# Reordering the paged decode of a hybrid decoder step, with operands of VectorE moved to PSUM

## The chip, the core and the metric

The kernel runs on one core of a Trainium2 chip. The metric is the device time of one execution in microseconds (us). TensorE (PE in the profile, PEld for its weight loads), VectorE (DVE), ScalarE (ACT), GpSimd (POOL) and the DMA queues of SyncE (SP) and ScalarE work side by side and meet at semaphores.

## The reference

One inference step of a two-layer decoder, all in float32, for a prompt of 16 + 512 tokens and 8 decode rows of one token each.

- Layer 0: a Mamba-2 mixer (`mamba2_mixer`), `post_norm`, a SwiGLU FFN (1024 to 2816 to 1024), `post_norm`. From its output come one set of keys and values for layer 1.
- Layer 1: differential attention over them (8 heads, two softmax maps each), `post_norm`, a second SwiGLU FFN, `post_norm`.
- The decode rows attend over paged past keys and values: per row 16 pages of 128 tokens, each page 128 x 1024 floats (512 KB) of keys and as much of values, so 128 pages of each, 134 MB in all.

```python
def post_norm(x, sub, w, b): return layer_norm(DEEPNORM_ALPHA * x + sub, w, b)
def swiglu(x, wg, wu, wd):   return (silu(x @ wg) * (x @ wu)) @ wd
def diff_attn_sample(h, k_past, v_past, k_new, v_new, ...):
    s = concat([einsum('bqhcd,bkhcd->bhcqk', q, k_past) * scale, s_new])
    w = softmax(s)[:, :, 0] - lam * softmax(s)[:, :, 1]
    o = w[..., :P] @ v_past + w[..., P:] @ v_new
```

## The kernel before

All 536 tokens (528 of the prompt, 8 decode rows) stand as columns; 1024 features are 8 tiles of 128 partitions. A float32 product is made of three matmuls on rounded halves: each operand is split into a high part (a ScalarE copy into the reduced type) and a low part (operand minus high part), and `unit` issues high-high, high-low and low-high (line 121). `wensure` (180) loads a weight chunk on ScalarE's DMA queue, makes its high part on ScalarE (200) and its low part (202) on the engine that `lo_engine` names: VectorE, and in the phase "attn" GpSimd. Four split chunks are kept.

The stages in order are the mixer, its output product, FFN 0 (`ffn`, 932; two parts of 11 gate/up pairs and 8 down products, at most 512 columns a matmul), the attention (`attention`, 1246; per head three products of keys, values and queries, then a generator `head`), the output product (`out_norm`, 1334), FFN 1 and the last norm. Each FFN's silu output is multiplied by the up product into SBUF (964) and then split there (`split`, 240).

`ln` (271) is a layer norm on column halves: sums over partitions by matmuls with ones, mean copied to SBUF (280), root by Ln and Exp (315); per pair of tiles a subtraction of the mean (288) and a product with the root (290), then per tile the high part on ScalarE (294), the value with weight and bias (303) and the low part (305). Norm 1 (`tight`) has lines 288 to 305 on VectorE and ScalarE; norms 0, 2 and 3 put some of 288, 303 and 305 on GpSimd.

A planner in the program sets the order. `Sched.t` adds a nominal time for each matmul that is emitted; generators (norms, heads, the decode) yield delays and are stepped when that clock passes them. A clock value is a place in the program's order, not a time on the chip. `finish(gen)` runs all that is due until a generator is done. SP's queue runs in the order of emission.

The decode first runs the whole layer 0 for the decode rows by itself (`early`, 1038), beside FFN 0, to get their queries; then `decode` (1154) is stepped every 3.2 of the planner's clock. Step n does key page n: a load into one of three slots (1151), the product with the query row on GpSimd (1191, in place, 128 x 1024), the sum over 64 features on VectorE (1192). It also does value page n - 24: a load into one of three other slots and four matmuls of 32 weight columns (the weights `w` of the row's softmax) into four quarters of the bank `ps_e` (1199; eight instructions in the trace). After 16 key pages a row's softmax is spawned (`dec_softmax`, 1208, four matmul and VectorE steps with yields of 0.6, 0.8 and 2.0); after 16 value pages `dec_out` (1232). The slots lie in the regions R5 and dA, which `out_norm` needs for the split attention output: it calls `S.finish(self.dec_gen)` at its start (1340).

Of the kernel before, what the change touches and what calls it, by code (L numbers as in the profile page):

```python
# [10 lines left out]
F32 = mybir.dt.float32  # L11
# [3 lines left out]
AF = mybir.ActivationFunctionType  # L15
# [21 lines left out]

ES0 = 24

KACT = (6, 7)  # L40
# [70 lines left out]
class Kernel:  # L111
# [68 lines left out]
    def wensure(self, load, split):  # L180
# [14 lines left out]
        while self.wsplit < min(split, len(self.wq)):  # L195
# [5 lines left out]
            eng = self.lo_engine()  # L201
            eng.tensor_tensor(out=lo[:, :n, :mw], in0=r, in1=hi[:, :n, :mw].bitcast(F32), op=ALU.subtract)  # L202
# [68 lines left out]
    def ln(self, t3, s2, q2, li, n, hilo=None, xf_out=None, after=None):  # L271
# [3 lines left out]
        pm, pv = (self.ps("c"), self.ps("d")) if n == NE else (self.ps(self.lnps[0]), self.ps(self.lnps[1]))  # L275
        self.mmf(pm[:, :n], self.ones, s2)
        self.mmf(pv[:, :n], self.ones, q2)
        md = self.sp.tile([P, 260], F32, tag="ln_md", name="ln_md")[:, :n]
        rs = self.sp.tile([P, 260], F32, tag="ln_rs", name="ln_rs")[:, :n]
        mdi = A.activation(md, pm[:, :n], AF.Copy, scale=1.0 / 1024)  # L280
        A.activation(rs, pm[:, :n], AF.Square, scale=1.0 / 1024)
        V.scalar_tensor_tensor(out=rs, in0=pv[:, :n], scalar=1.0 / 1024, in1=rs, op0=ALU.mult, op1=ALU.subtract)
        V.tensor_scalar(out=rs, in0=rs, scalar1=0.0, scalar2=None, op0=ALU.max)
        self.rsqrt(rs, rs, 1.0, mdi)
        for k in range(8):
            if k % 2 == 0:
                t2 = t3[:, k:k + 2, :]
                (G if k >= 4 and n > NE and not self.tight(li) else V).tensor_tensor(
                    out=t2, in0=t2, in1=bc(md, 1, 2), op=ALU.subtract)
                V.tensor_tensor(out=t2, in0=t2, in1=bc(rs, 1, 2), op=ALU.mult)  # L290
            w, b = self.lnw[:, li, k:k + 1], self.lnb[:, li, k:k + 1]
            if hilo is not None:
                hi, lo = hilo(k)
                A.activation(hi, t3[:, k, :], AF.Identity, bias=b, scale=w)
            if xf_out is not None:
                xf = xf_out(k)
            else:
                xf = self.sp.tile([P, LNW], F32, tag="lx", name="ln_xf", bufs=2)[:, :n]
            if (hilo is None and k % 2 == 0) or (self.tight(li) and k in KACT):
                A.activation(xf, t3[:, k, :], AF.Identity, bias=b, scale=w)  # L300
            else:
                E1 = V if self.tight(li) else G
                E1.tensor_scalar(out=xf, in0=t3[:, k, :], scalar1=w, scalar2=b, op0=ALU.mult, op1=ALU.add)  # L303
            if hilo is not None:
                (V if k % 2 == 0 or self.tight(li) else G).tensor_tensor(out=lo, in0=xf, in1=hi.bitcast(F32), op=ALU.subtract)  # L305
            if after is not None:
                after(k, xf)
# [4 lines left out]
    def tight(self, li):  # L312
        return li in (1,)

    def rsqrt(self, out, in_, scale, after=None):

        A = self.nc.scalar
        p = out.partition_size()
        l = A.activation(out, in_, AF.Ln, bias=self.eps[:p, :], scale=scale)
        e = A.activation(out, out, AF.Exp, scale=-0.5)  # L320
# [13 lines left out]
    def build(self):  # L334
        nc, tc = self.nc, self.tc
        with ExitStack() as ctx:
# [5 lines left out]
            self.gi, self.gn = 0, 3  # L342
            self.wi = 0
# [569 lines left out]
    def proj(self, groups, xk, halves, evac, lnf, lasth=None):  # L913
# [3 lines left out]
        for gi, grp in enumerate(groups):  # L917
            last = gi == len(groups) - 1
            chs = [self.wget(nc_) for _, nc_ in grp]
# [12 lines left out]
    def ffn(self, xk, halves, mk_t, lnf, gens, after_first=None, lasth=None, regs=("R0", "R1")):  # L932
# [3 lines left out]
        for part in range(2):  # L936
# [6 lines left out]
            while j < 11:  # L943
# [5 lines left out]
                for hf, (c0, n) in enumerate((lasth or halves) if first else halves):  # L949
# [4 lines left out]
                    for jj, (cg, cu) in zip(grp, chs):  # L954
# [83 lines left out]
    def early(self, t):  # L1038
# [106 lines left out]
        yield 3.0  # L1145
        self.dec_gen = S.spawn(self.decode(), 0.0)
# [7 lines left out]
    def decode(self):  # L1154
        nc, S, i, sp = self.nc, self.S, self.i, self.sp
        V, A, G = nc.vector, nc.scalar, nc.gpsimd
        kslot = self.kslot
        vslot = [self.r5[:, 1, :], self.r5[:, 2, :], self.r5[:, 3, :]]
# [4 lines left out]
        kq, vq = {}, {}  # L1163
        N = 128
# [6 lines left out]
        page = self.page  # L1171
        VL = 24
        w = {}
        sc = None
        qload(0)
        for n in range(N + VL + 1):
            if n < N:
                b, p = divmod(n, 16)
                if p == 8 and b < 7:
                    qload(b + 1)  # L1180
                if p == 0:
                    sc = sp.tile([P, 288], F32, tag="sc", name="sc", bufs=3)
                    V.memset(sc[:, 256:], 0.0)
                if n + 2 < N:
                    page("cache_k", n + 2, kslot[(n + 2) % 3])
            v = n - VL
            if 0 <= v + 2 < N:
                page("cache_v", v + 2, vslot[(v + 2) % 3])
            if n < N:
                kt = kslot[n % 3]  # L1190
                G.tensor_tensor(out=kt, in0=kt, in1=qslot[b % 2], op=ALU.mult)  # L1191
                V.reduce_sum(sc[:, 16 * p:16 * p + 16], kt.rearrange("p (c d) -> p c d", d=64), axis=AX)  # L1192
            if v >= 0 and v < N:
# [502 lines left out]
```

## Time and profile before

| | us |
|---|---|
| median of 3 runs (1810.86 to 1817.8) | 1814.14 |
| the profiled execution's own time | 1822.45 |
| its span, first to last instruction | 1820.6 |
| VectorE / ScalarE / GpSimd busy | 1170.4 / 731.7 / 567.0 |
| pages read by the decode | 256 of 512 KB |

The profiled execution is 8.3 us above the median. In the profile's windows FFN 0 with the decode beside it runs from about 605 to 980 us, the first head of the attention from about 1000, the last key/value/query product ends at 1319, the output product and norm 2 run to about 1430, FFN 1 to 1795. A busy share is an average over such stages; which wait ends last is read stage by stage.

### The profile page before, as it was taken

The numbers are of one execution on the slowest core, as the hardware profiler recorded it, in microseconds if no ns is written. First come the engines' busy times: TensorE is split into PE (matmuls) and PEld (weight loads), VectorE is DVE, ScalarE is ACT, GpSimd is POOL, SyncE is SP. The second block draws the span as 40 slices with busy tenths as digits, with TensorE's granted clock in tenths as the row PEclk, the third lists the DMA queues.
The fourth block names the chain that finished last, engine by engine and source line by source line (L and its number), as shares of the span: only waits on it lengthen the run. The fifth ranks groups of instructions, "written<-read, shape, count | busy, mean of one in ns | idle before, by whom it ended". The sixth has DMA issues, their size and how long they took to land.

```text
span 1820.6 us, 32047 instructions
## 1 busy us (share of the span) xinstructions
PE 1671.1 (92%) x12234; PEld 1408.3 (77%) x12234; DVE 1170.4 (64%) x1837; ACT 731.7 (40%) x1521; POOL 567.0 (31%) x402
## 2 busy tenths in 40 slices
PE   7899999979998989999997687999987899999996
PEld 7798888957775766666665464679976899999995
DVE  5498988934452699876678958757678533443334
ACT  6866765442442221222223222455644432223223
POOL 0010011001240586555588485312225400000025
PEclk9999999989999999999998697999998999999998
DMA  5665565596979779989898577761211222332221
GB/s 174 175 226 175 181 216 187 132 258 214 328 253 339 231 243 344 342 318 328 314 321 308 199 285 253 267 210 57 72 45 67 70 93 71 92 116 93 76 81 55
DMA packets 156800, 355.49 MB, mean 195 GB/s; under 512 B 23509, under 2 KB 74118, under 8 KB 156518
## 3 DMA queue, kind: packets, MB, share of 16 engines
q1 hardware_dynamic: 116902, 228.26, 37.6%
q10 hardware_dynamic: 36944, 116.59, 19.0%
q0 software_dynamic: 2800, 8.60, 1.4%
q8 instruction: 96, 1.57, 0.3%
q14 instruction: 58, 0.48, 0.1%
HBM read 337.07 MB, written 16.52 MB: 194 GB/s over the span
## 4 chain that ended last, share of the span: by engine, by line
PE 59%; DVE 17%; DMA 10%; ACT 5%; POOL 4%; issue 4%; SPq 1%; POOLq 0%; ACTq 0%; DVEq 0%
PE ps_g L121 48%; PE ps_e L125 3%; DMA st<-in_state_ssm 3%; DVE sc L1192 2%; PE ps_a L125 2%; DVE wlo L202 2%; PE ps_d L125 2%; DMA out_conv_s<-cv 1%; PE ps_c L125 1%; DMA dd<-in_cache_k 1%; POOL dd L1191 1%; POOL ln_xf L303 1%; ACT acsb L752 1%; DMA r<-in_w_out 1%; DMA r<-in_cache_v 1%
## 5 line engine op out<-in xcount | busy, mean ns | idle before, releaser
L200 ACT CAST whi<-raw 128x1024 fp32r<-128x1024 f32 (+3 forms) x243 | 234.8, 967 | 483.5 <-PE ps_g L121 419.2
L202 DVE TENSOR_TENSOR wlo<-raw,whi 128x1024 fp32r<-128x1024 f32 (+2 forms) x211 | 279.3, 1325 | 188.4 <-ACT whi L200 185.9
L1191 POOL TENSOR_TENSOR dd<-dd 128x1024 f32<-128x1024 f32 x85 | 216.3, 2550 | 97.7 <-DMA dd<-in_cache_k 88.1
L121 PE MATMUL ps_g<-xhi,whi 128*128 128x268 f32 (+1 forms) x656 | 196.8, 300 | 16.5 <-ACT xhi L242 9.2
L121 PE MATMUL ps_g<-x3hi,whi 128*128 128x260 f32 x704 | 200.4, 285 | 3.7 <-ACT sgw L958 3.2
L121 PE MATMUL ps_g<-x3lo,whi 128*128 128x260 f32 x704 | 199.6, 284 | 1.3 <-POOL x3lo L305 1.3
L121 PE MATMUL ps_g<-x3hi,wlo 128*128 128x260 f32 x704 | 199.2, 283 | 0.0
L121 PE MATMUL ps_g<-xhi,wlo 128*128 128x268 f32 (+1 forms) x656 | 194.4, 296 | 0.0
L121 PE MATMUL ps_g<-xlo,whi 128*128 128x268 f32 (+1 forms) x656 | 193.9, 296 | 0.1
L121 PE MATMUL ps_g<-x1hi,whi 128*128 128x512 f32 (+1 forms) x384 | 147.9, 385 | 4.1 <-ACT sgw L958 4.1
L121 PE MATMUL ps_g<-x1lo,whi 128*128 128x512 f32 (+1 forms) x384 | 148.5, 387 | 3.3 <-POOL x1lo L305 3.2
L121 PE MATMUL ps_g<-x1hi,wlo 128*128 128x512 f32 (+1 forms) x384 | 147.2, 383 | 0.0
L121 PEld LDWEIGHTS ps_g<-xhi,whi 128*128 128x128 f32 (+1 forms) x656 | 125.1, 191 | 24.3 <-ACT xhi L242 9.2
L1191 POOL TENSOR_TENSOR r<-r,dd 128x1024 f32<-128x1024 f32 x43 | 107.1, 2490 | 118.0 <-DMA dd<-scr_q 75.5
L121 PEld LDWEIGHTS ps_g<-x3hi,whi 128*128 128x128 f32 x704 | 133.0, 189 | 4.4 <-ACT sgw L958 3.6
L121 PEld LDWEIGHTS ps_g<-x3lo,whi 128*128 128x128 f32 x704 | 133.4, 189 | 1.5 <-POOL x3lo L305 1.5
L121 PEld LDWEIGHTS ps_g<-x3hi,wlo 128*128 128x128 f32 x704 | 133.7, 190 | 0.0
L121 PEld LDWEIGHTS ps_g<-xlo,whi 128*128 128x128 f32 (+1 forms) x656 | 125.3, 191 | 6.2 <-issue 5.1
L121 PEld LDWEIGHTS ps_g<-xhi,wlo 128*128 128x128 f32 (+1 forms) x656 | 125.0, 191 | 5.7 <-issue 5.1
L121 PE MATMUL ps_g<-hlo,whi 128*128 128x260 f32 (+2 forms) x400 | 126.7, 317 | 0.0
L121 PE MATMUL ps_g<-hhi,whi 128*128 128x260 f32 (+2 forms) x400 | 126.2, 316 | 0.0
L121 PE MATMUL ps_g<-hhi,wlo 128*128 128x260 f32 (+2 forms) x400 | 126.2, 316 | 0.0
(523 smaller groups left out, 4148.1 us busy)
## 6 DMA issues: line engine op xcount, KB each, us to landing
r<-in_cache_v SPq DMA_DIRECT2D x128, 512.0 KB, 5.3
dd<-in_cache_k SPq DMA_DIRECT2D x85, 512.0 KB, 4.6
raw<-in_w_gate ACTq DMA_DIRECT2D x44, 512.0 KB, 4.3
raw<-in_w_up ACTq DMA_DIRECT2D x44, 512.0 KB, 6.8
r<-in_cache_k SPq DMA_DIRECT2D x43, 512.0 KB, 6.5
raw<-in_w_in ACTq DMA_DIRECT2D x40, 512.0 KB, 3.6
raw<-in_w_down ACTq DMA_DIRECT2D x32, 384.0 KB, 3.2
raw<-in_w_down ACTq DMA_DIRECT2D x32, 320.0 KB, 4.7
```

Source lines behind the costliest of these rows:

```text
L121: return self.nc.tensor.matmul(out, lhsT=l, rhs=r, start=start, stop=stop)
L125: return self.nc.tensor.matmul(out, lhsT=l, rhs=r, start=start, stop=stop)
L200: nc.scalar.copy(hi[:, :n, :mw], r)
L202: eng.tensor_tensor(out=lo[:, :n, :mw], in0=r, in1=hi[:, :n, :mw].bitcast(F32), op=ALU.subtract)
L303: E1.tensor_scalar(out=xf, in0=t3[:, k, :], scalar1=w, scalar2=b, op0=ALU.mult, op1=ALU.add)
L752: A.activation(x, x, AF.Relu, scale=-1.0, bias=b)
L1191: G.tensor_tensor(out=kt, in0=kt, in1=qslot[b % 2], op=ALU.mult)
L1192: V.reduce_sum(sc[:, 16 * p:16 * p + 16], kt.rearrange("p (c d) -> p c d", d=64), axis=AX)
```

## The change

The decode walks all 128 key pages first, one page every 2.5 of the planner's clock, in five slots (the three of before and two that held values). A row's score tile gets a place of its own for all eight rows. Then come all 128 value pages, two every 4.8, in seven slots (those five and the two of the query rows), the four matmuls of a page with one priority. The softmax yields longer delays.

While `wps` is set (from the decode's start to the last group of FFN 0) the low part of a weight chunk is made in two halves: ScalarE copies a half of the raw chunk to PSUM bank a or b, and VectorE subtracts with that operand. The gate-times-up product is written into the PSUM bank of the up product and split from there, in both FFNs. The norms read mean and root from PSUM and fold weight and bias in another way; only the bias of half the tiles of norm 3 stays on GpSimd. The phase "attn", and with it GpSimd's low parts, begins after head 0's products.

```diff
+KY, VY = 2.5, 4.8
@@ wensure
-            eng = self.lo_engine()
-            eng.tensor_tensor(out=lo[:, :n, :mw], in0=r, in1=hi[:, :n, :mw].bitcast(F32), op=ALU.subtract)
+            if self.wps:
+                for x in range(0, n, 4):
+                    y = min(x + 4, n)
+                    pw = self.ps("ab"[x // 4])[:, :P * (y - x)].rearrange("p (k c) -> p k c", c=P)
+                    nc.scalar.copy(pw, r[:, x:y, :])
+                    nc.vector.tensor_tensor(out=lo[:, x:y, :], in0=pw, in1=hi[:, x:y, :].bitcast(F32), op=ALU.subtract)
+            else:
...
@@ ln
-        mdi = A.activation(md, pm[:, :n], AF.Copy, scale=1.0 / 1024)
...
-        self.rsqrt(rs, rs, 1.0, mdi)
+        self.rsqrt(pv, rs, 1.0, sqi, mid=rs)
+        for k in range(0, 8, 2):
+            t2 = t3[:, k:k + 2, :]
+            V.scalar_tensor_tensor(out=t2, in0=bc(pm, 1, 2), scalar=-1.0 / 1024, in1=t2, op0=ALU.mult, op1=ALU.add)
         for k in range(8):
-            if k % 2 == 0:
-                t2 = t3[:, k:k + 2, :]
-                (G if k >= 4 and n > NE and not self.tight(li) else V).tensor_tensor(
-                    out=t2, in0=t2, in1=bc(md, 1, 2), op=ALU.subtract)
-                V.tensor_tensor(out=t2, in0=t2, in1=bc(rs, 1, 2), op=ALU.mult)
             w, b = self.lnw[:, li, k:k + 1], self.lnb[:, li, k:k + 1]
+            t = t3[:, k, :]
+            V.scalar_tensor_tensor(out=t, in0=t, scalar=w, in1=pv, op0=ALU.mult, op1=ALU.mult)
             if hilo is not None:
                 hi, lo = hilo(k)
-                A.activation(hi, t3[:, k, :], AF.Identity, bias=b, scale=w)
...
+                A.activation(hi, t, AF.Identity, bias=b)
+                V.scalar_tensor_tensor(out=lo, in0=t, scalar=b, in1=hi.bitcast(F32), op0=ALU.add, op1=ALU.subtract)
+            else:
                 xf = xf_out(k)
...
+                if small or k % 2 == 0:
+                    A.activation(xf, t, AF.Identity, bias=b)
+                else:
+                    G.tensor_scalar(out=xf, in0=t, scalar1=b, scalar2=None, op0=ALU.add)
@@ ffn
-                        V.tensor_tensor(out=sg, in0=sg, in1=pu[:, :n], op=ALU.mult)
+                        V.tensor_tensor(out=pu[:, :n], in0=sg, in1=pu[:, :n], op=ALU.mult)
                         hh, hl = hk(jj)
-                        self.split(hh[:, c0:c0 + n], hl[:, c0:c0 + n], sg)
+                        self.split(hh[:, c0:c0 + n], hl[:, c0:c0 + n], pu[:, :n])
@@ decode (rewritten)
+        kslot = self.kslot + [self.r5[:, 1, :], self.r5[:, 2, :]]
+        N, R = 128, 5
...
+        for n in range(N):
+            b, p = divmod(n, 16)
...
+            if n + R - 1 < N:
+                self.page("cache_k", n + R - 1, kslot[(n + R - 1) % R])
+            kt = kslot[n % R]
+            G.tensor_tensor(out=kt, in0=kt, in1=qslot[b % 2], op=ALU.mult)
+            V.reduce_sum(w[b][:, 16 * p:16 * p + 16], kt.rearrange("p (c d) -> p c d", d=64), axis=AX)
+            yield KY
...
+        vslot = [kslot[n % R] for n in range(N - R, N)] + qslot
+        R = 7
+        for n in range(R - 2):
+            self.page("cache_v", n, vslot[n])
+        yield 6.0
+        for n in range(N):
...
+            if n + R - 2 < N:
+                self.page("cache_v", n + R - 2, vslot[(n + R - 2) % R])
...
+            pr = self.tc.cur_priority
+            for j in range(4):
+                self.tc.cur_priority = pr
+                self.mmf(pe[32 * j:32 * j + 32, :256], w[bv][:, 16 * pv:16 * pv + 32],
+                         vt[:, 256 * j:256 * j + 256], start=pv == 0, stop=pv == 15, share=4)
...
+            if n % 2 == 1:
+                yield VY
@@ dec_softmax, dec_out: yields 0.6, 0.8, 2.0 become 2.5, 2.5, 4.0; 1.0 becomes 2.0
@@ attention
-        self.phase = "attn"
...
                     for wi in range(3):
                         kvq(h, wi, chs[wi], hf)
+                self.phase = "attn"
```

## Rows read from the trace of the kernel before

**Rows 1.** The page, part 1: busy us, share of the span, instructions.
```profile
PE 1671.1 (92%) x12234; PEld 1408.3 (77%) x12234; DVE 1170.4 (64%) x1837; ACT 731.7 (40%) x1521; POOL 567.0 (31%) x402
```

**Rows 2.** Windows by stage: us, busy us and (instructions) per engine; clock, DMA share, GB/s.
```profile
605.00:755.00 150.00, 139.76 (x674) 102.30 (x673) 136.40 (x116) 35.57 (x46) 109.44 (x43) 0.99 0.84 294
755.00:955.00 200.00, 200.00 (x1085) 136.53 (x1084) 138.75 (x131) 55.40 (x70) 126.47 (x54) 1.00 0.90 320
980.00:1055.00 75.00, 49.52 (x320) 36.26 (x320) 67.93 (x83) 27.02 (x49) 42.18 (x19) 0.70 0.64 222
1055.00:1130.00 75.00, 54.61 (x420) 39.96 (x419) 61.67 (x103) 17.52 (x46) 50.33 (x28) 0.82 0.74 260
1130.00:1320.00 190.00, 182.13 (x1546) 153.72 (x1543) 125.29 (x324) 101.14 (x347) 55.49 (x38) 0.97 0.45 158
1320.00:1430.00 110.00, 88.09 (x633) 80.86 (x632) 83.45 (x187) 52.58 (x141) 48.77 (x44) 0.91 0.15 51
1430.00:1795.00 365.00, 364.17 (x3031) 363.84 (x3030) 141.93 (x225) 102.36 (x173) 23.95 (x30) 1.00 0.27 86
```

**Rows 3.** The same windows, line 121 (split matmuls) alone.
```profile
605.00:755.00 150.00, 128.73 (x524) 97.89 (x523) 0.99 0.84 294
755.00:955.00 200.00, 175.33 (x698) 126.77 (x697) 1.00 0.90 320
980.00:1055.00 75.00, 35.35 (x200) 31.13 (x200) 0.70 0.64 222
1055.00:1130.00 75.00, 38.77 (x266) 33.52 (x265) 0.82 0.74 260
```

**Rows 4.** The same windows, accumulator ps_e alone (8 instructions are one value page).
```profile
605.00:755.00 150.00, 10.86 (x136) 2.67 (x136) 0.00 (x0) 0.37 (x1) 0.99 0.84 294
755.00:955.00 200.00, 29.39 (x368) 7.24 (x368) 0.00 (x0) 0.75 (x2) 1.00 0.90 320
980.00:1055.00 75.00, 10.97 (x104) 2.32 (x104) 0.00 (x0) 0.36 (x1) 0.70 0.64 222
1055.00:1130.00 75.00, 12.12 (x128) 2.84 (x128) 0.00 (x0) 0.37 (x1) 0.82 0.74 260
1180.00:1205.00 25.00, 7.64 (x88) 1.86 (x88) 0.00 (x0) 0.00 (x0) 1.00 0.88 294
```

**Rows 5.** TensorE in order of time: start us, us, what, count.
```profile
828.67 0.39 PE L121 MATMUL ps_g<-x1hi,whi 128*128 128x512 f32 x1
828.99 0.64 PE L125 MATMUL ps_e<-r,sc 128*32 128x256 f32 x8
829.56 0.50 PE L121 MATMUL ps_g<-x1lo,whi 128*128 128x512 f32 x1
829.89 0.39 PE L121 MATMUL ps_g<-x1hi,wlo 128*128 128x512 f32 x1
1083.53 1.07 PE L125 MATMUL ps_e<-r,sc 128*32 128x256 f32 x16
1318.85 0.28 PE L121 MATMUL ps_g<-x2hi,wlo 128*128 128x264 f32 x1
```

**Rows 6.** VectorE groups by form: count, busy us, mean ns, idle before.
```profile
L202 DVE TENSOR_TENSOR wlo<-raw,whi 128x1024 fp32r<-128x1024 f32 x37 | 60.3, 1629 | 12.8 <-ACT whi L200 12.0
L202 DVE TENSOR_TENSOR wlo<-raw,whi 128x1024 fp32r<-128x1024 f32 x40 | 48.9, 1224 | 56.5 <-ACT whi L200 56.5
L964 DVE TENSOR_TENSOR sgw<-sgw,ps_g 128x512 f32<-128x512 f32 x11 | 7.5, 686 | 20.4 <-PE ps_g L121 20.4
```

**Rows 7.** Lines 1191, 1192 and 305: count, ns min/median/max, first and last start.
```profile
L1191 POOL TENSOR_TENSOR dd<-dd x85: 2342/2406/3391, 607.0 to 1150.6; 128x1024 f32<-128x1024 f32 x85
L1192 DVE TENSOR_REDUCE sc<-dd x85: 1174/1206/1222, 610.9 to 1159.4; 128x16 f32<-128x1024 f32 x85
L305 DVE TENSOR_TENSOR x2lo<-ln_xf,x2hi x16: 403/411/2576, 1009.6 to 1044.4; 128x256 fp32r<-128x256 f32 x16
```

**Rows 8.** A GpSimd group by form: count, busy us, mean ns, idle before.
```profile
L303 POOL TENSOR_SCALAR ln_xf<-t,c_ln_w,c_ln_b 128x256 f32<-128x256 f32 x16 | 15.1, 951 | 7.7 <-DVE t L290 6.3 <-DVE x1lo L305 1.2
```

More of the change, by code (lines that the diff above doesn't have):

```diff
@@ L296, in ln @@
                 xf = xf_out(k)
[L297 to L305, printed above, removed]
@@ L315, in rsqrt @@
-    def rsqrt(self, out, in_, scale, after=None):
+    def rsqrt(self, out, in_, scale, after=None, mid=None):
         A = self.nc.scalar
         p = out.partition_size()
-        l = A.activation(out, in_, AF.Ln, bias=self.eps[:p, :], scale=scale)
-        e = A.activation(out, out, AF.Exp, scale=-0.5)
+        mid = out if mid is None else mid
+        l = A.activation(mid, in_, AF.Ln, bias=self.eps[:p, :], scale=scale)
+        e = A.activation(out, mid, AF.Exp, scale=-0.5)
         if after is not None:
@@ L918, in proj @@
             last = gi == len(groups) - 1
+            if last and lnf:
+                self.wps = False
             chs = [self.wget(nc_) for _, nc_ in grp]
@@ L1162, in decode, with room @@
         self.oT = sp.tile([P, 8, 16], F32, name="oT", tag="oT")
-        kq, vq = {}, {}
-        N = 128
+        N, R = 128, 5
+        w, st = [], {"h": None}
+        def room(b):
+            if b < 3:
+                sc = sp.tile([P, 288], F32, tag="sc", name="sc", bufs=3)
+            elif b < 6:
+                sc = self.r5[:, 3, 288 * (b - 3):288 * (b - 2)]
+            else:
+                if b == 6:
+                    st["h"] = sp.tile([P, 2, 288], F32, name="sch", tag="hE")
+                sc = st["h"][:, b - 6, :]
+            V.memset(sc[:, 256:], 0.0)
+            return sc
         def qload(b):
@@ L1169, in qload @@
                                                             ap=[[0, P], [1, 1024]]))
[L1171 to L1174, printed above, removed]
         qload(0)
[L1176 to L1193, printed above, removed]
-                bv, pv = divmod(v, 16)
-                if pv == 0:
-                    pe = self.ps("e")
-                vt = vslot[v % 3]
-                for j in range(4):
-                    self.mmf(pe[32 * j:32 * j + 32, :256], w[bv][:, 16 * pv:16 * pv + 32],
-                             vt[:, 256 * j:256 * j + 256], start=pv == 0, stop=pv == 15, share=4)
-                if pv == 15:
-                    S.spawn(self.dec_out(bv, pe), 0.5)
-            yield 3.2
-            if n < N and p == 15:
-                w[b] = sc
-                S.spawn(self.dec_softmax(b, sc), 0.0)
@@ new lines, in decode @@
+        for n in range(2, R - 1):
+            self.page("cache_k", n, kslot[n % R])
+        for n in range(N):
+            b, p = divmod(n, 16)
+            if p == 8 and b < 7:
+                qload(b + 1)
+            if p == 0:
+                w.append(room(b))
+            if n + R - 1 < N:
[4 more added lines that the diff above has]
+            yield KY
+            if p == 15:
+                S.spawn(self.dec_softmax(b, w[b]), 0.5)
```

41 lines of the change are left out of this document (23 added, 18 removed).

## The prediction

> **What bounds the kernel now.** I read the page's busy shares first, then windows by stage, then the matmuls in order of time, last the groups of single lines. TensorE is busy 92% of the span [rows 1], so what matters is where it is not fed. In the window from 1430 us on, FFN 1, it never idles: 3031 matmuls in 365 us, 0.120 us each at 256 to 264 columns [rows 2]. Nothing of the change can shorten that stage or the mixer before 605 us, which the change hardly touches.
>
> Between 605 and 1430 us I compare each window with what its matmuls need. From 755 to 955 us TensorE has no idle time either. It runs 698 split matmuls of 512 columns, 46 value pages of 8 instructions and 19 others (at 0.2 us, 4 us) [rows 2 to 4]. Two starts of split matmuls around a page lie 1.22 us apart (828.67 to 829.89), and they hold two split matmuls and the page [rows 5]. With a for the one and b for the other, 698a + 46b = 196 and 2a + b = 1.22 give a = 0.231 us and b = 0.76 us. By these prices:
>
> - 605 to 755: 524 x 0.231 + 17 pages x 0.76 + 14 x 0.2 = 137 of 150 us, 13 lost [rows 2 to 4]
> - 980 to 1055 (norm 1 and head 0's products): 200 x 0.12 + 13 x 0.76 + 16 x 0.2 = 37 of 75, 38 lost, at a clock of 0.70 [rows 2 to 4]
> - 1055 to 1130 (head 0 begins): 266 x 0.12 + 16 x 0.76 + 26 x 0.2 = 49 of 75, 26 lost, clock 0.82 [rows 2 to 4]
> - 1130 to 1320: the 30 pages that are left of 128 (240 of its 1546 instructions), 30 x 0.76 + 1306 x 0.12 = 180 of 190, 10 lost [rows 2, 4]
> - 1320 to 1430 (output product, last heads, norm 2): 633 x 0.12 = 76 of 110, 34 lost, clock 0.91 [rows 2]
>
> So about 120 us could be won in all, and 64 of them stand between 980 and 1130 us, where VectorE is busy 68 and 62 of 75 us [rows 2]. Why it is so busy there shows in line 305: the same subtraction takes 411 ns at the median and 2576 ns at most [rows 7]. The weight's low part takes 1629 ns on the mean while GpSimd multiplies key pages, and 1224 ns in FFN 1, where it doesn't [rows 6]. The product of line 964, one of whose operands is in PSUM, takes 686 ns for 512 columns beside the same GpSimd work [rows 6]. A VectorE instruction with both operands in SBUF is held by a GpSimd one; with one operand in PSUM it is not.
>
> **The change part by part.** The sum is made against the profiled execution's own 1822.45 us.
>
> *The order of the pages.* The number of value pages is the same, so 128 x 0.76 us of TensorE only move: the 63 pages between 605 and 955 us [rows 4], and those up to 980, leave FFN 0 and come back in the attention. That is 0 in the sum. FFN 0 gets shorter by some 50 us and the attention longer by as much.
>
> *Pairs.* Sixteen instructions in one train took 1.07 us [rows 5]; one page alone took 0.57 from its start to the next split matmul, and its neighbours 0.19 more. A pair then costs 1.07 + 0.19 = 1.26 against 1.52, and 64 pairs save 17 us at most. In the attention some neighbours are short float32 matmuls that hide the switch already. I take -10 (bounds -17 and 0).
>
> *FFN 0 with keys alone.* A chunk of 24 matmuls moves the planner by 24 x 512 / 2400 = 5.12 and takes 24 x 0.231 = 5.54 us, so a key page every 2.5 of the planner's clock comes every 2.7 us. GpSimd needs 2.41 us for it at the median [rows 7], 89% of its time, and its running sums of the last down products come on top. VectorE needs 1.21 us for the page's sum [rows 7]; per two chunks (11.1 us) that is 4.1 pages, 5.0 us, then four PSUM halves of low parts and lines 964 and 243, six at 0.686, 4.1 us, and 0.9 for softmax: 10 of 11.1 us. ScalarE's copies into PSUM (two of about 0.6 us a chunk, like its other 512-column instructions) lie in an engine that was busy 91 of 350 us [rows 2]. So three engines stand near 90% together. The 13 us that 605 to 755 loses, with VectorE busy 136 of 150 [rows 2], should go; as much is lost anew, when a sum waits for GpSimd and a low part behind it on VectorE's queue waits too. I take 0. Below is -13 (nothing lost). Above, the loss of 605 to 755, 13 on 137 us, holds for all of FFN 0's 125 pages x 2.7 = 337 us and grows as the pages stand closer, 3.2 / 2.5: 41 us, of which 13 are there now, +28.
>
> *Norm 1 and head 0 without keys.* The keys end, by the planner, at 128 x 2.5 = 320 after the decode's start. Adding the planner's constants along the program gives 350 to the attention's start before; less 85 value pages at 0.43 that is 314. So keys end with FFN 0. VectorE loses the key sums there (each step did one page of either kind, so 13 + 16 = 29 [rows 4], 35 us of the 130 that it is busy), its stretched instructions shrink to the median, and per half of the norm it has 4 x 0.686 + 16 x 0.41 = 9.3 us to do (the products and the low parts [rows 6, 7]), with 66 down matmuls of the other half, 8 us, beside it. Of the 64 us lost I expect 24 to stay: about 5 for each half of the norm, 14 for head 0, whose rotation, maximum and softmax are a chain. -40, with bounds -60 and -5 (nothing but shorter sums).
>
> The Trainium skill has a rule for this, in SBUF — State Buffer, section Who interferes with whom: a VectorE instruction with two SBUF inputs contends with a GpSimd instruction that reads SBUF, and the one that comes second waits for the whole of the other. The trace agrees: 2576 ns is 411 plus most of a 2406 ns key product [rows 7]. By the rule a PSUM half costs 0.686 us whatever GpSimd does; if all of VectorE's work were stretched instead, by 1629 / 1224 [rows 6], the six instructions of two chunks would take 5.5 us, not 4.1, VectorE would need 11.4 of 11.1 us, and FFN 0 would be some 10 us longer. The rule also speaks against one edit: the norm's new low part still has both operands in SBUF, so key pages that slip into norm 1 hold it up to 2.2 us each time; six of them would add 13 us, inside the range above.
>
> *Norms 0, 2 and 3.* Their GpSimd steps (line 303 at 951 ns, eight per half [rows 8], the subtractions and four low parts) go to VectorE at 9.3 us per half. GpSimd is off the chain of norms 0 and 2; norm 3 keeps four bias steps there. Six halves at 1 us each: -6 (bounds -15 and +4, if VectorE's longer row of steps is the later end).
>
> *The gate product in PSUM.* It holds the up product's bank about 1.5 us longer, and the next unit that wants it comes two units later, 5 us or more. 0 in FFN 1, where TensorE never waits [rows 2].
>
> *The tail of the values.* By the planner values end at 320 + 6 + 64 x 4.8 = 633. `out_norm` begins at 569 before (350 + 219 along the program), and at the same 569 after, since the sum of matmuls is unchanged. 64 / 2.4 = 27 pages are left when the last head's products are out, and the output product cannot start before they are read, because its operand lies in their slots. Before, it began at once (at 1319 [rows 5]) and ran beside the last two heads, 76 us of matmuls in 110. After, 27 pages come at the speed of the loads: at the 320 GB/s of 755 to 955 [rows 2] a page is 1.64 us, 44 us in all, with heads 6 and 7 beside them; the output product then has TensorE for itself: 44 + 76 = 120. +10. At the rate of 1180 to 1205 us, 11 pages in 25 us [rows 4], it is 62 us, +28. Below is 0, if the last heads alone need as long.
>
> Sum: -10 + 0 - 40 - 6 + 10 = -46: 1776 for an execution like the profiled one, 8.3 less, 1768 us, for the median of runs.
>
> **The rivals.**
>
> *The tail decides, and the kernel is slower.* Pages are loaded from SP's queue in the program's order, among key and value outputs that wait for a head's rotation, and heads 6 and 7 are still in it. 29 pages took 150 us while norm 1 and head 0 ran, 5.2 us each, and 11 took 25 us later, 2.3 each [rows 4]. Halfway, at 3.8 us, 27 pages are 103 us, 59 more than I counted: -46 + 59 = +13, 1827 at the median. It decides from (44 + 46) / 27 = 3.3 us a page on. Against it: seven slots instead of three, and 11 pages in 25 us when the planner asked for them.
>
> *GpSimd sets FFN 0.* The upper end above, +28, so -18, 1796. For it: three engines at 90%, and queues in order. Against it: five slots take away the wait for pages.
>
> *The attention is held by its own chains.* The loss between 980 and 1130 us stays, because a norm and a head's softmax are latencies and not VectorE's load; -5 in place of -40: -11, 1803. For it: 190 us of heads run nearly full only once two are in flight [rows 2]. Against it: VectorE busy 130 of 150 us.
>
> *Values fill the heads.* With a pair always due, TensorE has work in each gap, also in 1130 to 1320 and beside heads 6 and 7 (10 and 34 lost): 30 more, -76, 1738.
>
> **How the numbers follow.** Chances: the forecast 0.55, GpSimd's pace 0.15, own chains 0.10, values as filler 0.07, the slower tail 0.13. About 0.5% (9 us) is what a measurement can tell from no change; faster means under 1805, slower over 1823. The forecast, GpSimd's pace, the filler and half of the chains are faster, 0.82, less 0.03 for their upper ends: 0.79. Slower is the tail but for 0.02, which like the rest falls within 0.5%: 0.11 and 0.10. The lower ends lie 7, 13, 20, 9 and 10 us below what I took, 59 in all; three quarters of that are 46, so the range begins at 1722. It ends at 1818, beyond the own chains, and leaves out the slow tail and the very best.
>
> **What would show each step.** Value matmuls absent before FFN 0's last down product and in trains of 16 after it. Low parts at two halves of 0.69 us beside key products. FFN 0 shorter by 45 to 55 us, with GpSimd busy near 90%. Norm 1 and head 0 with 20 to 30 us lost, at a clock above 0.85. A stretch after the last query product in which TensorE has value pages alone: 35 to 60 us. The prediction is wrong if that stretch is over 90 us, if FFN 0 is not at least 25 us shorter, or if the window after it loses over 50 us.

## The result and the profile after

The changed kernel is slower: 1834.94 us at the median of 15 runs (1824.17 to 1843.84) beside 1819.43 (1810.86 to 1829.49) for the kernel before on the same chip. The ratio is 1.0085, with a 95% interval of 1.0064 to 1.0106. Forecast were 1768 us and a range up to 1818. The profiled execution's span is 1835.4 us, 14.8 above that of before.

Places in the program, read from TensorE's row of both traces, show where the time stands (start of the matmul, us from the span's start; for the last x1 and x3 the last one on the operand's low part, 0.1 to 0.2 us ahead of the very last):

| | before | after | difference |
|---|---|---|---|
| last x1 matmul (gate and up products of FFN 0 done) | 909.4 | 908.5 | -0.9 |
| first x2 matmul (head 0) | 999.2 | 1009.0 | +9.8 |
| last x2 matmul (all queries, keys, values) | 1318.9 | 1309.6 | -9.3 |
| first matmul of the output product | 1319.0 | 1344.8 | +25.9 |
| first x3 matmul (FFN 1) | 1411.0 | 1432.3 | +21.2 |
| last x3 matmul | 1736.5 | 1753.3 | +16.8 |
| span | 1820.6 | 1835.4 | +14.8 |

Up to the last x1 matmul FFN 0 lost all of its value pages and did not get shorter. From there to the last query product the kernel won 8 us although 102 value pages stand there now instead of 76: 11 us were lost up to head 0 and 19 won behind it. Then 30 us were lost up to FFN 1. FFN 1 and the last norms gave back 6.

The page of the kernel after, part 1 (columns as in [rows 1]):

```profile
PE 1678.7 (91%) x12234; PEld 1421.6 (77%) x12234; DVE 1149.6 (63%) x1955; ACT 788.3 (43%) x1646; POOL 485.9 (26%) x337
```

Windows of the kernel after, with the stretches and columns of [rows 2]:

```profile
605.00:755.00 150.00, 135.88 (x563) 108.52 (x562) 132.75 (x152) 60.63 (x99) 130.11 (x54) 0.94 0.79 275
755.00:955.00 200.00, 173.74 (x713) 137.85 (x711) 184.76 (x186) 90.40 (x136) 168.52 (x75) 0.94 0.75 262
980.00:1055.00 75.00, 58.24 (x453) 44.44 (x452) 58.74 (x120) 30.56 (x73) 26.35 (x18) 0.84 0.59 224
1055.00:1130.00 75.00, 73.44 (x647) 52.46 (x646) 36.93 (x107) 30.86 (x103) 13.00 (x11) 1.00 0.65 244
...
1430.00:1795.00 365.00, 364.05 (x2999) 363.62 (x3000) 150.26 (x248) 107.75 (x186) 14.48 (x19) 0.99 0.27 87
```

Read these against [rows 2]. From 755 to 955 TensorE had no idle time before; now it is busy 173.74 of 200 us, at a clock of 0.94 instead of 1.00, with 713 matmuls instead of 1085. VectorE's busy time rose from 138.75 to 184.76 us and GpSimd's from 126.47 to 168.52. The next two windows, 980 to 1130, are where the forecast expected its gain, and TensorE is fuller there: 58.24 and 73.44 us busy instead of 49.52 and 54.61, clock 0.84 and 1.00 instead of 0.70 and 0.82. FFN 1 is as full as it was.

Windows with fixed ends mix stages that have shifted. Here are those from the last x1 matmul to the first x2 one and on to the last x2 one, first of the kernel before, then of the kernel after:

```profile
909.40:999.20 89.80, 81.30 (x514) 57.77 (x512) 68.55 (x67) 27.06 (x42) 73.14 (x36) 0.96 0.89 313
999.20:1318.90 319.70, 274.46 (x2189) 221.37 (x2186) 235.09 (x489) 135.09 (x422) 134.91 (x78) 0.88 0.55 193
```

```profile
908.50:1009.00 100.50, 77.00 (x424) 59.49 (x422) 84.19 (x103) 35.33 (x63) 76.50 (x39) 0.86 0.70 246
1009.00:1309.60 300.60, 292.23 (x2497) 222.36 (x2497) 156.57 (x427) 130.34 (x425) 58.04 (x46) 0.99 0.58 219
```

Up to head 0 TensorE's idle time grew from 8.5 to 23.5 us; from head 0 on it fell from 45.2 to 8.4, at a clock of 0.99 instead of 0.88.

VectorE's groups by form in the kernel after, 605 to 909 us (count, busy us, mean ns, idle before):

```profile
L1204 DVE TENSOR_REDUCE r<-r 128x16 f32<-128x1024 f32 x30 | 36.1, 1209 | 3.3 <-POOL r L1203 3.3
...
L206 DVE TENSOR_TENSOR wlo<-ps_a,whi 128x512 fp32r<-128x512 f32 x49 | 33.2, 677 | 3.3 <-ACT whi L200 3.2
...
L1242 DVE TENSOR_SCALAR d_dg<-c_ident,d_m 16x16 f32<-16x16 f32 x6 | 23.8, 3960 | 0.1
...
L1247 DVE TENSOR_TENSOR r<-r,Mb 128x256 f32<-128x256 f32 x3 | 20.6, 6853 | 0.1
L914 DVE SCALAR_TENSOR_TENSOR t<-x1lo,t 128x512 f32<-128x512 f32 x8 | 15.9, 1985 | 0.0
L262 DVE TENSOR_TENSOR t<-t,stk 128x512 f32<-128x512 f32 x8 | 13.3, 1666 | 0.0
```

The low parts do what the forecast said: with one operand in PSUM a half takes 677 ns beside GpSimd's products, so a chunk 1354 ns, against 1629 ns before [rows 6]. The page sums are untouched, 1209 ns. But line 1242, which multiplies a 16x16 identity by a maximum for the decode's softmax, takes 3960 ns on the mean, and line 1247, which subtracts that maximum from 128x256 scores, 6853 in the three of this row. Both have all of their operands in SBUF. One such place in order of time, first VectorE, then GpSimd, then TensorE (start us, us, what, count, idle before):

```profile
942.97 1.20 DVE L1204 TENSOR_REDUCE sch<-dd 128x16 f32<-128x1024 f32 x1
944.09 14.11 DVE L1242 TENSOR_SCALAR d_dg<-c_ident,d_m 16x16 f32<-16x16 f32 x1
958.12 0.67 DVE L206 TENSOR_TENSOR wlo<-ps_a,whi 128x512 fp32r<-128x512 f32 x1
```

```profile
942.78 2.44 POOL L1203 TENSOR_TENSOR dd<-dd 128x1024 f32<-128x1024 f32 x1
945.15 1.33 POOL L276 TENSOR_TENSOR stq<-stq,sgw 128x512 f32<-128x512 f32 x1
946.40 4.74 POOL L1203 TENSOR_TENSOR r<-r,dd 128x1024 f32<-128x1024 f32 x2
951.06 1.30 POOL L275 TENSOR_TENSOR sts<-sts,t 128x512 f32<-128x512 f32 x1
952.28 2.38 POOL L1203 TENSOR_TENSOR r<-r,dd 128x1024 f32<-128x1024 f32 x1
954.57 2.38 POOL L1203 TENSOR_TENSOR dd<-dd 128x1024 f32<-128x1024 f32 x1
956.87 1.30 POOL L276 TENSOR_TENSOR stq<-stq,sgw 128x512 f32<-128x512 f32 x1
964.77 2.60 POOL L1203 TENSOR_TENSOR dd<-dd 128x1024 f32<-128x1024 f32 x1 [6.59 <-DMA dd<-in_cache_k]
```

```profile
948.50 0.39 PE L121 MATMUL ps_g<-hhi,whi 128*128 128x512 f32 x1
948.73 0.40 PE L121 MATMUL ps_g<-hlo,whi 128*128 128x512 f32 x1
958.25 0.60 PE L125 MATMUL ps_c<-d_dg,ones 16*128 16x16 f32 x2 [9.12 <-DVE d_dg L1242]
958.79 0.80 PE L121 MATMUL ps_g<-hhi,wlo 128*128 128x512 f32 x1
```

The 256 numbers of line 1242 wait 14.11 us, from 944.09 to 958.20. GpSimd runs its products and running sums without a gap from 942.78 until 958.17, eight instructions; the step on VectorE gets through when that row stops. The row stops because it has run out of pages: the next product waits 6.59 us for a load, and a load needs a slot, which only a page's sum on VectorE, queued behind line 1242, sets free. On TensorE the softmax's own small matmul stands at the head of the queue and waits 9.12 us for line 1242 with FFN 0's matmuls behind it. The next matmul takes 0.80 us; those ahead of the wait took 0.40.

Not every such step waits so long. Here line 1242 met a product too, and the next one followed without a gap, but the step was through after 1.04 us (VectorE, then GpSimd):

```profile
844.29 1.04 DVE L1242 TENSOR_SCALAR d_dg<-c_ident,d_m 16x16 f32<-16x16 f32 x1
```

```profile
842.87 7.18 POOL L1203 TENSOR_TENSOR r<-r,dd 128x1024 f32<-128x1024 f32 x3
```

Counted over lines 1242, 1247, 914 and 262, from 605 to 1000 us: 25 steps met a GpSimd instruction under way, and in 17 cases the next one followed at once. In 12 of these the step got in behind the first; in five it was passed over, and then it waited each time (9.42 to 14.11 us) until GpSimd paused for a page. What decides between the two isn't shown.

TensorE's longest waits, kernel after, 605 to 1009 us (total us, times, longest):

```profile
PE ps_c L125 <- DVE d_dg L1242: 21.5, 4, 9.1
PE ps_c L125 <- ACT r L1248: 11.0, 2, 6.5
PE ps_e L125 <- DMA r<-in_cache_v: 10.7, 3, 9.0
PE ps_g L121 <- DVE wlo L206: 7.5, 1, 7.5
```

The second line is the exponential that waits for line 1247, the fourth a weight's low part that is queued behind steps of line 262. The third is of another kind, the load of the first value pages.

The other loss, windows of the kernel after around the last query product:

```profile
1130.00:1310.00 180.00, 175.57 (x1514) 132.60 (x1516) 85.30 (x241) 78.57 (x269) 31.84 (x27) 1.00 0.57 213
1310.00:1345.00 35.00, 28.63 (x286) 11.78 (x278) 14.71 (x47) 11.18 (x45) 2.48 (x2) 0.85 0.92 373
1345.00:1432.00 87.00, 65.33 (x441) 60.53 (x442) 63.74 (x136) 30.25 (x70) 22.86 (x20) 0.83 0.17 55
```

In the 35 us to 1345 the DMA engines are busy 0.92 of the time at 373 GB/s; 26 value pages (208 instructions) come there as fast as they can be loaded, 1.3 us each. Before that, in the 180 us to 1310, the DMA share is 0.57.

### The profile page after: what moved, and what is told of

It reads as the page before. It is cut to its first block, busy times and chain, and to the rows that moved or that the text cites. A ratio compares the mean times of both kernels' runs of the same rounds, so it can differ in the third digit from the quotient of the medians.

```text
span 1835.4 us, 32166 instructions
## 1 busy us (share of the span) xinstructions
PE 1678.7 (91%) x12234; PEld 1421.6 (77%) x12234; DVE 1149.6 (63%) x1955; ACT 788.3 (43%) x1646; POOL 485.9 (26%) x337
## 4 chain that ended last, share of the span: by engine, by line
PE 59%; DVE 18%; DMA 10%; ACT 6%; issue 3%; POOL 1%; SPq 1%; ACTq 0%; POOLq 0%; DVEq 0%
PE ps_g L121 47%; PE ps_e L125 4%; PE ps_a L125 2%; DMA st<-in_state_ssm 2%; DVE d_dg L1242 2%; DMA dd<-in_cache_v 2%; DVE wlo L206 1%; ACT acsb L755 1%; PE ps_b L121 1%; PE ps_c L125 1%; DVE r L1204 1%; DVE sc L1204 1%; DVE r L1247 1%; PE ps_d L125 1%; DMA r<-in_cache_v 1%
## 5 line engine op out<-in xcount | busy, mean ns | idle before, releaser
L209 DVE TENSOR_TENSOR wlo<-raw,whi 128x1024 fp32r<-128x1024 f32 (+3 forms) x148 | 175.9, 1190 | 152.4 <-ACT whi L200 151.4
L1203 POOL TENSOR_TENSOR r<-r,dd 128x1024 f32<-128x1024 f32 x76 | 185.0, 2459 | 41.2 <-DMA r<-in_cache_k 37.6
L1203 POOL TENSOR_TENSOR dd<-dd 128x1024 f32<-128x1024 f32 x52 | 127.1, 2463 | 124.8 <-PE ps_g L121 110.9
L209 POOL TENSOR_TENSOR wlo<-raw,whi 128x1024 fp32r<-128x1024 f32 (+1 forms) x31 | 70.3, 2268 | 301.0 <-ACT whi L200 285.0
```

## The experiments

Twelve kernels (rows 2 to 13 of the table), each compared with the kernel before on its own chip. In the table: the ratio with its 95% interval; VectorE's time in FFN 0's steps with all operands in SBUF (lines 1242, 1247, 914 and 262 of the kernel after, page sums left out, from 605 us to the last x1 matmul; their plain time is in it); and three of the places above. The places are of one profiled execution each: in after, vy36 and single36, whose FFN 0 is the same program, the last x1 matmul differs by 15 us, so that much is no finding there.

| kernel | ratio | SBUF-only steps, us | last x1 | last x2 | first x3 |
|---|---|---|---|---|---|
| after | 1.0085 [1.0064, 1.0106] | 75.9 | 908.5 | 1309.6 | 1432.3 |
| sm_off | 0.9929 [0.9900, 0.9959] | 32.1 | 881.6 | 1277.6 | 1400.3 |
| r3 | 1.0085 [1.0057, 1.0112] | 35.0 | 895.0 | 1310.9 | 1433.5 |
| r4 | 1.0058 [1.0028, 1.0087] | 43.1 | 889.3 | 1295.1 | 1417.4 |
| vy36 | 0.9939 [0.9909, 0.9969] | 65.7 | 904.1 | 1308.9 | 1403.8 |
| single36 | 0.9980 [0.9951, 1.0009] | 75.8 | 919.1 | 1331.8 | 1423.9 |
| oldnorm | 1.0018 [0.9985, 1.0051] | 50.9 | 884.3 | 1288.1 | 1408.0 |
| combo1 | 0.9799 [0.9746, 0.9852] | 34.1 | 883.3 | 1292.7 | 1385.9 |
| combo2 | 0.9704 [0.9668, 0.9740] | 0 | 870.1 | 1267.4 | 1362.4 |
| combo3 | 0.9725 [0.9682, 0.9767] | 0 | 870.2 | 1270.4 | 1360.6 |
| c2_oldnorm | 0.9734 [0.9686, 0.9781] | 0 | 863.5 | 1260.5 | 1351.9 |
| c2_r3 | 0.9942 [0.9916, 0.9968] | 0 | 890.3 | 1308.8 | 1403.7 |
| lp_only (from before) | 0.9998 [0.9971, 1.0025] | | 910.0 | 1318.0 | 1411.0 |

**sm_off: the softmax's two steps moved off SBUF-only operands.**

```diff
-        V.tensor_scalar(out=dg, in0=self.ident[:16, :16], scalar1=m1, scalar2=None, op0=ALU.mult)
+        A.activation(dg, self.ident[:16, :16], AF.Copy, scale=m1)
...
-        V.tensor_tensor(out=s3, in0=s3, in1=bc(self.Mb[:, b, :], 1, 16), op=ALU.subtract)
+        V.tensor_tensor(out=s3, in0=s3, in1=bc(pc[:, :16], 1, 16), op=ALU.subtract)
```

> The kernel after, with the softmax's two VectorE steps that had all their operands in SBUF taken off them: the 16x16 diagonal is made by ScalarE, and the subtraction of the maximum reads the maximum from its PSUM bank. Theory A (a VectorE instruction with SBUF operands alone waits while GpSimd multiplies key pages back to back, and all of VectorE's queue behind it): the diagonal and the subtraction, together 47 us in FFN 0, fall to under 1 us each; the last x1 matmul comes at 865 to 885 us instead of 908.5; the kernel is 25 to 45 us faster than the changed one, 1790 to 1812. Theory B (three engines near 90% and queues in order; the long softmax steps only take up slack that VectorE has anyway): the last x1 matmul at 895 us or later, the time within 12 us of the changed kernel. Theory C (the low parts' two PSUM halves, each waiting for ScalarE's copy, set the pace): like B.

1808.52 us, some 26 under the changed kernel (by the ratios 1.5%). Line 1247 in this run (ns min/median/max):

```profile
L1247 DVE TENSOR_TENSOR sc<-sc,ps_c x3: 406/409/410, 664.4 to 765.8; 128x256 f32<-128x256 f32 x3
L1247 DVE TENSOR_TENSOR r<-r,ps_c x3: 408/410/410, 798.8 to 876.8; 128x256 f32<-128x256 f32 x3
```

The same 256 columns that took up to 10604 ns now take 410 at most, with GpSimd busier than in the changed kernel (253.75 of 276.6 us up to the last x1 matmul, against 253.38 of 303.5). Last x1 comes 27 us earlier and the gain is kept to the end. Theory A's figures hold; B and C, which wanted 895 or later, fall. One long step is left in this trace, in the residual of the down products, VectorE and then GpSimd beside it:

```profile
685.65 11.02 DVE L914 SCALAR_TENSOR_TENSOR t<-x1lo,t 128x512 f32<-128x512 f32 x1
```

```profile
682.06 4.80 POOL L1203 TENSOR_TENSOR r<-r,dd 128x1024 f32<-128x1024 f32 x2
686.80 4.72 POOL L1203 TENSOR_TENSOR dd<-dd 128x1024 f32<-128x1024 f32 x2
691.46 4.65 POOL L1203 TENSOR_TENSOR r<-r,dd 128x1024 f32<-128x1024 f32 x2
```

**r3 and r4: three and four key slots, nothing else.** What matters of the diff (r4 likewise):

```diff
-        N, R = 128, 5
+        N, R = 128, 3
```

> The kernel after with three key slots instead of five, and nothing else. Theory A (starvation by back-to-back key products): a page's load then ends later than the product before it more often, GpSimd's row has gaps, and the diagonal and the subtraction take under 5 us at most instead of 14.1 and 10.6; the last x1 matmul between 880 and 900 us, if the later pages do not cost more themselves. Theory B: GpSimd, busy near 90% already, only loses by the gaps: the last x1 matmul at 908 or later, the time equal to the changed kernel or up to 20 us slower.

> The kernel after with four key slots. Theory A with its length: a VectorE step without a PSUM operand waits until GpSimd has no page left whose load is done, so the longest wait grows with the slots: 2.5 us with three (one product), 10.6 to 14.1 with five; with four 4.5 to 8 us (two or three products). Last x1 matmul 890 to 905. Rival: the wait is one product with any number of slots, and the 14 us came of the running sums that GpSimd also does: then four slots show about 2.5 in FFN 0's first part, or as much as five.

Lines 1242 and 1247 with three slots:

```profile
L1242 DVE TENSOR_SCALAR d_dg<-c_ident,d_m x8: 211/798/2376, 665.0 to 1048.2; 16x16 f32<-16x16 f32 x8
```

```profile
L1247 DVE TENSOR_TENSOR sc<-sc,Mb x3: 543/1281/2431, 672.2 to 775.6; 128x256 f32<-128x256 f32 x3
L1247 DVE TENSOR_TENSOR r<-r,Mb x3: 1479/1974/2505, 824.1 to 922.0; 128x256 f32<-128x256 f32 x3
```

With three slots no step waits longer than 2505 ns, one product. With four, the longest before the running sums begin is this one, and GpSimd's row beside it:

```profile
833.99 4.98 DVE L1242 TENSOR_SCALAR d_dg<-c_ident,d_m 16x16 f32<-16x16 f32 x1
```

```profile
834.28 4.67 POOL L1203 TENSOR_TENSOR r<-r,dd 128x1024 f32<-128x1024 f32 x2
840.27 2.39 POOL L1203 TENSOR_TENSOR dd<-dd 128x1024 f32<-128x1024 f32 x1 [1.32 <-DMA dd<-in_cache_k]
```

That is 4.98 us, two products, ended by GpSimd's wait for a page; with five slots 9.42 to 10.60 us, four. So the longest wait goes with the slots, as theory A said (its last x1 of 890 to 905 was 889.3), though with four slots it is this one step: 17 of 19 that met two products in a row got in behind the first. One step in r4 took 11.89 us, more than it said: it fell among the running sums of FFN 0's last down products, which are in GpSimd's row too and need no slot. In time three slots win nothing: FFN 0 is 14 us shorter in this trace, no more than the spread, and all of it is lost again. The last key product starts at 1027.4 instead of 982.5, and the values end later with it. Theory B's time came out, for another reason than B's.

**vy36: a pair of value pages every 3.6 instead of 4.8.**

```diff
-KY, VY = 2.5, 4.8
+KY, VY = 2.5, 3.6
```

> The kernel after with a pair of value pages every 3.6 of the planner's clock instead of 4.8, so that by the planner the values end with the last head's products. Theory T (the 35 us between the last query product and the output product are pages that were asked for too late, loaded at the full rate of the DMA engines): the last value matmul comes within 10 us of the last query product, which itself comes 5 to 15 us later; FFN 1 begins 10 to 20 us earlier, 1815 to 1827. Theory U (the pages wait in SP's queue behind the heads' outputs, whatever the planner asks): the last value matmul stays 25 us or more behind the last query product, and the time stays within 6 us of the changed kernel.

1814.47 us, theory T, half a microsecond under its range. Windows of this kernel around the same place:

```profile
1030.00:1130.00 100.00, 99.68 (x928) 69.62 (x927) 51.17 (x143) 41.78 (x133) 20.79 (x16) 1.00 0.93 344
1130.00:1310.00 180.00, 176.68 (x1610) 132.15 (x1607) 88.87 (x244) 81.06 (x266) 34.59 (x27) 1.00 0.67 242
1310.00:1345.00 35.00, 30.32 (x225) 27.29 (x223) 25.06 (x78) 14.69 (x53) 6.00 (x4) 0.90 0.09 28
```

The pages are loaded beside the heads (DMA share 0.93 to 1130), the last value matmul stands at 1284.3, and the output product begins at 1309.0, right behind the last query product. From the first to the last x2 matmul it took 304.3 us instead of 300.6: 26 more pages cost the heads 4 us, not the 5 to 15 expected.

**lp_only: the kernel before with the low parts through PSUM, and no more of the change.** The diff is the first hunk of the change.

> The kernel before with one part of the change alone: low parts in FFN 0 by ScalarE's copy into PSUM and two halves on VectorE. Theory C (this step costs FFN 0 what the change lost there): last x1 matmul 10 to 40 us later than the 909.4 of before, the kernel slower by 10 us or more. Theory A: the step alone is harmless or a gain, since TensorE idled only 10 us of 304 there before: last x1 matmul between 898 and 912, time within 12 us of before or faster by up to 12.

No difference in time (0.9998), last x1 at 910.0. The step is harmless, and without denser key pages it gains nothing either. Theory C falls.

**combo1: sm_off and vy36 together.**

> The kernel after with both mended: softmax's two steps off SBUF-only operands, and a pair of value pages every 3.6. The two alone measured 26 and 20 us under the changed kernel. If the two losses are separate (theories A and T), they add up: last x1 matmul at 882, first x3 about 1370 to 1378, time 1784 to 1794. If FFN 0's gain only makes the pages wait elsewhere (they are asked for sooner while the loads run at the same rate), less than 35 us of the 46 come: 1800 or more.

1786.19 us: the gains add up (26 and 20 under 1835 would be 1788). The last x1 matmul came where it was expected, the first x3 one at 1385.9, 8 us behind the end of its range.

**combo2: the residual and FFN 0's last low parts too.** The core of the edit beside combo1:

```diff
+                    V.scalar_tensor_tensor(out=p, in0=xl, scalar=ALPHA, in1=p, op0=ALU.mult, op1=ALU.add)
+                    if m > 0:
+                        V.tensor_tensor(out=p, in0=p, in1=kv, op=ALU.subtract)
+                    V.scalar_tensor_tensor(out=tv, in0=xh, scalar=ALPHA, in1=p, op0=ALU.mult, op1=ALU.add)
...
             chs = [self.wget(nc_) for _, nc_ in grp]
+            if last and lnf:
+                self.wps = False
```

Here p is the product's own PSUM bank, so that each step has one operand there, and the switch back to low parts without PSUM stands behind the last chunks instead of ahead of them.

> As combo1, with two more SBUF-only rows of VectorE beside the key products turned into PSUM ones: FFN 0's residual and shift (in the run with the mended softmax one of them still took 11.02 us, and the 16 took 32 us against 11 at the plain price), and the low parts of its last down chunks (five at 3.3 us there). Theory A in full: the window 655 to 705, which still lost 11 us, fills, and last x1 comes at 865 to 873; the norm's start 8 to 12 us earlier still; time 10 to 22 us under combo1. Theory A only for softmax (its chain through TensorE and ScalarE is what made its stalls cost; others are hidden): under 6 us.

1766.12 us, 20 under combo1; of that 13 before the last x1 and 7 to 8 more at the first x2. This is the version that beats both kernels, by 3.0% and 3.8% (0.9704 / 1.0085 = 0.962). Windows of combo2 in FFN 0:

```profile
655.00:705.00 50.00, 44.11 (x178) 34.73 (x177) 41.66 (x59) 21.98 (x38) 50.00 (x22) 0.93 0.83 277
705.00:870.00 165.00, 165.00 (x716) 132.76 (x715) 143.12 (x191) 86.64 (x135) 158.99 (x68) 1.00 0.91 323
```

The stretch to 705 was to fill and still loses 6 us. From 705 to 870 TensorE is busy all of the time, with GpSimd at 159 of 165 us and VectorE at 143. So three engines near 90% do go together; what did not was a VectorE step with two SBUF operands.

**single36: vy36 with one page at a time.**

```diff
-            if n % 2 == 1:
-                yield VY
+            yield VY / 2
```

> As vy36, but one value page every 1.8 of the planner's clock instead of two every 3.6. The forecast priced a page alone at 0.76 us and a pair at 1.26, 17 us in 64 pairs: 1824 to 1832 against vy36's 1814. Rival: the pages' neighbours hide the switch, or pages stand in trains anyway: within 5 us of vy36.

Its FFN 0, which the edit does not touch, ended 15 us later in the profiled execution than vy36's, so I compare behind it: from the first x2 to the first output product 308.3 us against 304.4. The medians differ by 3.4 us, the ratios by 0.4% (7 us), with intervals that overlap. Of 17 us about 4 came behind FFN 0. TensorE's row says why: in vy36 the pages stand alone between other matmuls too, 112 groups of eight instructions of `ps_e` against five of sixteen and two of twenty-four.

**oldnorm and c2_oldnorm: the norm of before in the kernel after and in combo2.**

> The kernel after with the norm of before. Forecast's term: the rewritten norm was to save a part of 40 us in norm 1 and 6 us in the other norms. If it does its work: 6 to 25 us slower than the changed kernel (1841 to 1860), of it 4 to 15 between the last x1 matmul and the first x2 one. Rival: once the key products are gone from norm 1 the old norm is as quick, within 5 us of the changed kernel.

> As combo2, but with the norm of before. In the changed kernel the old norm measured 0.67% less, yet its FFN 0 ended 24 us earlier, with 47 us of stretched VectorE steps instead of 76, and its norm stages were not shorter. If that was only where the long steps fell (the norm itself is a small gain): with those steps gone the old norm is 4 to 15 us slower than combo2's 1766, last x1 within 5 us of 870. If the new norm itself costs time: it is faster than combo2, under 1762.

In the kernel after the old norm measured less (1.0018), in combo2 the same within the intervals (0.9734 and 0.9704). From the first to the last x3 matmul the new norm takes 320.1 us against 324.8 in the pair of combo2, and that is all that repeats of it; up to the first x3 the old norm's run was ahead by 10. Neither expectation came: the rewritten norm is worth nothing that the runs can tell, and its larger time in the changed kernel goes with 75.9 against 50.9 us of waiting steps. Why these fell less badly with the old norm stays open; three of 23 were passed over there, against five of 17.

**combo3: combo2 with the values starting later (16 instead of 6).**

> As combo2, with the first value page 16 instead of 6 of the planner's clock after the last key page. In combo2 TensorE's queue stands 12.3 us before norm 1 at the first value page's load, with the norm's sums and a softmax behind it. If that wait is what norm 1 loses: first x2 matmul 5 to 12 us earlier, time 1754 to 1762. Rival: VectorE is late there on its own (a low part takes 8.1 us beside the last key products), and the norm ends when it did: within 3 us of combo2.

1766.40 us, no difference; the first x2 stayed at 961.9. But the edit did not do what it was for: TensorE still waits 11.1 us for the first value page, instead of 12.3, and that page's matmul starts at 944.9 instead of 946.1. So the time fits the rival, and what this wait costs norm 1 stays open.

**c2_r3: combo2 with three key slots.**

> As combo2 with three key slots. Tells what five slots bring once no VectorE step is starved. In the changed kernel three slots made FFN 0 14 us shorter, but the keys ended later and all of it was lost in the attention. If more slots are a gain by themselves (GpSimd never waits for a page): 8 to 25 us slower than combo2. If not, within 5 us.

1808.07, 42 us slower. Five slots are worth 42 us once no VectorE step waits for GpSimd, more than expected; in the kernel after, where three slots cost nothing, the waiting steps took that gain away.

## Why the prediction was wrong

- *FFN 0 with keys alone, 0 (-13 to +28).* This step failed. The last x1 matmul was to come earlier by the pages that stood ahead of it, and it stood where it was. Those pages are 52, 17 up to 755 us [rows 4] and 35 in this row of the kernel before, accumulator `ps_e`:

```profile
755.00:909.00 154.00, 22.36 (x280) 5.51 (x280) 0.00 (x0) 0.75 (x2) 1.00 0.89 320
```

At 0.76 us they are 40 us (the 50 of the forecast has the pages up to 980 in it), and 39 of them did not come. The three engines' shares were near (in combo2 GpSimd 96%, VectorE 87%), and so were the low parts' price and the page's. What I missed is a coupling between them: I priced a VectorE step with SBUF operands at the whole of one GpSimd instruction at most, and took VectorE's softmax steps at 0.9 us per two chunks. With five slots GpSimd often has the next product ready, and then such a step can wait for four of them, or eight instructions with running sums between. sm_off took 27 us of it away, combo2 another 11 to 13 with the residual; the 870.1 reached is 39 us under before, all of what the pages were worth.

- The Trainium skill, in SBUF — State Buffer, section Who interferes with whom, says that the instruction which comes second waits for the whole of the other. r3 agrees, with 2505 ns at most and products of 2.4 us. With five slots the trace agrees for 12 steps of 17 and differs for five, up to 14.11 us behind eight instructions, and the measurement decides. The section also says that a VectorE instruction with at most one SBUF input does not contend with GpSimd, the 2-port modes aside. The trace agrees: with one operand in PSUM, 410 ns in sm_off for what took 10604.
- *GpSimd's pace*, the rival with +28, named the right place and the wrong reason; its upper end was also too small. It had no waiting step in it.
- *Tail of the values, +10 (0 to +28).* Too small: the last x2 to the first x3 took 92.2 us before and 122.7 after, +30.5. That 122.7 stands close to the 120 that I had worked out is in part luck: the pages alone took 35 us, 1.3 us each (44 forecast, and well under the 3.3 from which my slower rival decided), and the output product and norm behind them 87.5 instead of 76. The wrong size was the stage of before: I set it at 110 us, a window that ended at 1430, while FFN 1 began at 1411. The cause, pages asked for too late, is shown by vy36.
- *The order of the pages, 0.* The sum has an error here: TensorE's time for the 27 pages of the tail, 20 us at 0.76, comes back in the attention by this term and is once more in the tail's 44 us. By its own prices the forecast was about -66.
- *Norm 1 and head 0, -40.* Right in size and wrong in place. From the first x2 matmul to the last the stage got 19 us shorter with 38 more pages, 29 us at 0.76: 48 won, beside the 50 of this term and the pairs. But from the last x1 matmul to the first x2 one it got 10.7 us longer with 12 pages fewer, 20 worse than forecast. Two waits of TensorE stand there, 9.12 us for line 1242 and 9.04 for the first value page; what the second costs stays open. The gain came of the keys' leaving: the norm's new form showed none of its own.
- *Pairs, -10.* Nothing to 4 us; the pages do not stand in trains of 16. *Norms 0, 2 and 3, -6*: 4 to 5 us in FFN 1's stretch, but no gain in the whole. *Low parts, gate product, 0*: as priced.
- *Values as filler*, the rival at 0.07, was right in its mechanism and not in this kernel: vy36 put 26 more pages beside the heads for 4 us.

The sum by places: forecast -46, without the pages counted twice -66; FFN 0 to the last x1 matmul +39; on to the first x2 one +20; heads +2; the tail +20; measured about +15. Of the signs named for a wrong prediction one came: FFN 0 was not 25 us shorter.

With both losses mended combo2's profiled span, 1764.6, stands 56 us under before's. That its median of 1766 lies beside the forecast's 1768 is luck: it has edits that the forecast did not price, and the forecast counted pages twice.

## What to carry to other kernels

Beside a GpSimd that never pauses, look at every VectorE step with two SBUF operands, the smallest too, and reckon with GpSimd's whole unbroken row, not with one instruction; one operand in PSUM or the step on ScalarE takes the price away. More buffers for a producer can lengthen that row, so that they can cost as much as they bring. Where work is moved behind another stage, set its cost against the stage's end as read from the chain's last and first instructions, not against a window, and count the time of moved work in one place only.

## What the runs showed of the hardware

- A waiting VectorE step with two SBUF operands can be passed over by a GpSimd instruction that is ready at once: in five of 17 such cases in the changed kernel, two of 19 with four slots, none of ten with three. The longest step took 2.5 us with three slots and, ahead of the running sums, 4.98 with four and 10.60 with five; with running sums between 11.89 with four and 14.11 with five. Each that was passed over ended when GpSimd paused. Page sums (`TENSOR_REDUCE`, one SBUF operand) were never held: 1196 to 1223 ns.
- The price on TensorE is under the wait itself. From 75.9 us of SBUF-only steps (last x1 at 908.5) to none (870.1) it is 0.51 us per us; in the other runs with five slots, against the same 870.1, 0.28 to 0.65 (rough, since equal programs differ by 15 us in the last x1). TensorE idles, and the granted clock of FFN 0's windows falls from 0.99 and 1.00 to 0.94.
